# First product of two squared-ReLU MLPs by one level of Strassen's algorithm, their activations through DRAM

## The chip, the core and the metric

The kernel runs on one core of one Trainium2 chip. The metric is the device time of one execution in microseconds (us). Three runs of the kernel before took 2856.18, 2854.34 and 2856.22 us; the median is 2856.18 us.

## What is computed

An encoder trunk of two layers on 1024 tokens with 1024 features, in float32. Each layer is a token mixer and an MLP, both with a pre-RMSNorm and a residual add:

```python
def rmsnorm(x, w):
    y = xf * lax.rsqrt(jnp.mean(xf * xf, axis=-1, keepdims=True) + EPS)
    return y * w
def sq_relu_mlp(h, w1, w2):          # w1: 1024 x 4096, w2: 4096 x 1024
    a = jax.nn.relu(h @ w1)
    return (a * a) @ w2
h = x
h = h + neighbourhood_attention(rmsnorm(h, na_norm), na_w_qkv, na_rpb, na_w_o)
h = h + sq_relu_mlp(rmsnorm(h, mlp_norm[0]), mlp_w1[0], mlp_w2[0])
h = h + gated_deltanet(rmsnorm(h, gdn_norm), gdn_w_in, ..., gdn_w_o)
h = h + sq_relu_mlp(rmsnorm(h, mlp_norm[1]), mlp_w1[1], mlp_w2[1])
return rmsnorm(h, final_norm)
```

## The kernel before, in words

Features lie on the 128 partitions and tokens along the free dimension, so a feature tile is 128 x 1024 and is worked on in two halves of 512 tokens. Every float32 operand is split into two float32r tiles, `hi` (a rounded copy) and `lo` (the rest), and a product of 128 x 128 weights with 128 x 512 tokens is three matmuls: hi hi, hi lo, lo hi (`product`, line 120, its matmul on line 132). ScalarE (ACT) makes `hi`, VectorE (DVE) makes `lo`.

Weights come by `weight` (line 91): per 512 rows x 128 columns one DMA of 256 KB on SyncE's queue (SP) into a `wraw` buffer (three), then `split_w` (line 104): a cast to `whi` on ACT (line 108) and a subtraction to `wlo` on DVE (line 109), with three buffers each. One such split is used by 4 k-tiles x 3 matmuls x 2 halves = 24 matmuls.

The order of the instructions on each engine is not the order of the program text: the framework schedules by the program's order as priority, and an instruction whose inputs and buffers are ready is put ahead of an earlier one that is not. What has a buffer to go to can run ahead.

Around the MLPs the work is staged so. `out_proj` (line 509) makes the mixer's output projection: 8 feature tiles x 2 halves; in layer 0 over 8 k-tiles, in layer 1 over the last 2 heads only (the other six were added to the residual in DRAM during the mixer). The residual tiles `h` (8 tiles of 512 KB) were brought from DRAM by `unspill` (line 527). Each half is added from PSUM to `h` on DVE (line 518), and `norm_tile` (line 142) makes hi (ACT, line 152) and lo (DVE, line 153) of gain * h, the squares (ACT, line 163) and their running sum on GpSimd (POOL, line 164). The factor 1/sqrt(mean) per token, being the same for all features, is only put in after the first product: `norm_end` (line 194) with its sums over partitions (line 178), a power on POOL (line 170) and its spread over the partitions (line 190).

`mlp` (line 198) takes 4 blocks of 1024 hidden features. A block first makes 8 hidden tiles: for each tile and half, 24 matmuls with `w1`, then `max(ps, 0) * rstd` (DVE, line 221), its square as `ahi` (ACT, line 222), the square once more on POOL (line 223) and `alo` (DVE, line 224). The hidden tiles stay in SBUF, in one of two sets of 16 slots called X and A (the other holds the MLP's input). Then the block makes its part of the second product, 8 output tiles x 2 halves x 24 matmuls with `w2`, and adds each to `h` (DVE, line 250; in the last block `after` follows with the next norm, the spill to DRAM or, in layer 1, the final norm and the output).

Either product of one MLP is 32 x 2 x 24 = 1536 matmuls. PSUM has 8 banks: two `mm` banks rotate for the products, two `pa` banks serve the norms.

## Time and profile before

| what | value |
|---|---|
| median of three runs | 2856.18 us |
| span of the profiled execution (no other time of it is given) | 2853.0 us |
| PE busy | 2782.4 us, 14844 matmuls |
| DVE busy | 1377.4 us, 2905 instructions |
| ACT busy | 938.7 us, 2111 instructions |
| POOL busy | 604.7 us, 871 instructions |
| DMA | 177.13 MB, mean 62 GB/s |

PE is TensorE's matmul, PEld its weight load. A row of the windows view gives, for a stretch of the span in us from its start, its length, then the busy time and the instructions of PE, PEld, DVE, ACT and POOL, the granted clock of TensorE, the DMA engines' busy share and the rate. A row of the groups gives line, engine, operation, out<-in, count, then busy us and mean ns of one, then the idle time before them and what ended it. A row of the timeline gives start, duration, engine, line, operation and count. Neighbouring matmuls overlap in the records, so the pace of PE is read from counts in a stretch, not from the duration of one.

MLP 0's `out_proj` runs from about 525 to 605 us, its blocks to about 1335 us; MLP 1's `out_proj` begins at 2076.5 us, its blocks about 2111 us.

### The profile page before, as it was taken

Reading aid. Unit: us, or ns where it says so; the run is one execution under the profiler, and the core shown is the slowest. Engines: PE = TensorE matmul, PEld = TensorE weight load, DVE = VectorE, ACT = ScalarE, POOL = GpSimd, SP = SyncE. Lnnn points to the kernel's source line nnn. Section 1 sums busy time; section 2 is a strip of 40 time slices with the busy share of each in tenths; the row PEclk is TensorE's granted clock in tenths of the full one; section 3 lists DMA queues with packets and bytes.
Section 4 is the critical chain, followed back from the end, with each engine's and each line's share of the span. In section 5 each row is a group of like instructions: output and inputs, shape, how many; then the busy total and the mean of one; then the engine's idle time right before and its main releaser. Section 6 shows DMA issues by size and latency. Waiting matters only on the chain. (4 is left out here: it accounts for less than half of the span.)

```text
span 2853.0 us, 39344 instructions
## 1 busy us (share of the span) xinstructions
PE 2782.4 (98%) x14844; PEld 2198.5 (77%) x14844; DVE 1377.4 (48%) x2905; ACT 938.7 (33%) x2111; POOL 604.7 (21%) x871
## 2 busy tenths in 40 slices
PE   8999999999999999999998999899989999999998
PEld 6766666788888888877777878787868888888887
DVE  5155556433232232334767888887563232232333
ACT  5144444332121121223445555455342121121134
POOL 0101111121010010112155545543142011020111
PEclk9999999999999999999999999999999999999999
DMA  7212212221111111123112222114331111111123
GB/s 194 53 44 58 52 45 51 96 60 49 48 45 51 45 48 49 45 71 91 43 41 51 53 53 50 43 43 117 114 117 50 45 48 49 45 49 48 45 70 115
DMA packets 308588, 177.13 MB, mean 62 GB/s; under 512 B 75054, under 2 KB 286638, under 8 KB 308398
## 3 DMA queue, kind: packets, MB, share of 16 engines
q1 hardware_dynamic: 299982, 166.13, 20.6%
q0 software_dynamic: 3072, 8.39, 1.3%
q8 instruction: 117, 1.92, 0.3%
q10 hardware_dynamic: 5344, 0.09, 0.1%
q14 instruction: 73, 0.60, 0.1%
HBM read 141.62 MB, written 24.55 MB: 58 GB/s over the span
## 5 line engine op out<-in xcount | busy, mean ns | idle before, releaser
L132 PE MATMUL mm<-X,whi 128*128 128x512 f32 x2800 | 902.2, 400 | 0.9 <-ACT X L499 0.7
L132 PE MATMUL mm<-A,whi 128*128 128x512 f32 (+1 forms) x2124 | 669.9, 396 | 3.3 <-ACT whi L108 1.9
L132 PEld LDWEIGHTS mm<-X,whi 128*128 128x128 f32 x2800 | 525.3, 188 | 132.2 <-issue 7.5
L132 PE MATMUL mm<-X,wlo 128*128 128x512 f32 x1400 | 559.7, 400 | 0.0
L132 PEld LDWEIGHTS mm<-A,whi 128*128 128x128 f32 x2124 | 398.9, 189 | 100.0 <-ACT whi L108 2.9
L108 ACT CAST whi<-wraw 128x512 fp32r<-128x512 f32 (+1 forms) x338 | 208.0, 616 | 792.6 <-PE mm L132 760.1
L132 PE MATMUL mm<-A,wlo 128*128 128x512 f32 (+1 forms) x1062 | 419.8, 396 | 2.5 <-DVE wlo L109 2.5
L1189 PE MATMUL mm<-A,whi 128*128 128x512 f32 x1216 | 404.5, 413 | 1.1 <-DVE A L1189 1.1
L223 POOL TENSOR_TENSOR r<-r 128x512 f32<-128x512 f32 x128 | 152.1, 1188 | 1104.6 <-DVE r L221 1098.5
L109 DVE TENSOR_TENSOR wlo<-wraw,whi 128x512 fp32r<-128x512 f32 (+1 forms) x338 | 243.3, 721 | 199.0 <-ACT whi L108 198.6
L132 PEld LDWEIGHTS mm<-X,wlo 128*128 128x128 f32 x1400 | 263.8, 188 | 63.0 <-issue 1.7
L1189 PEld LDWEIGHTS mm<-A,whi 128*128 128x128 f32 x1216 | 214.8, 191 | 41.4 <-DVE A L1189 1.9
L1189 PE MATMUL mm<-A,wlo 128*128 128x512 f32 x608 | 241.6, 397 | 0.0
L132 PEld LDWEIGHTS mm<-A,wlo 128*128 128x128 f32 x1062 | 200.6, 189 | 50.3 <-DVE wlo L109 3.4
L221 DVE SCALAR_TENSOR_TENSOR r<-mm,rs 128x512 f32<-128x512 f32 x128 | 88.5, 691 | 287.7 <-PE mm L132 286.8
L250 DVE TENSOR_TENSOR h<-mm,h 128x512 f32<-128x512 f32 x111 | 76.7, 691 | 300.4 <-PE mm L132 300.4
L1189 POOL TENSOR_TENSOR xt<-lp,xi 128x126 f32<-128x126 f32 (+22 forms) x248 | 110.4, 445 | 174.5 <-DMA lp<-dsc 155.7
L1189 DVE SCALAR_TENSOR_TENSOR X<-xp,cw,X 128x512 f32<-128x512 f32 x192 | 141.9, 780 | 1.7 <-ACT X L1189 1.0
L1189 PEld LDWEIGHTS mm<-A,wlo 128*128 128x128 f32 x608 | 115.3, 190 | 28.0
L164 POOL TENSOR_TENSOR rs<-rs,r 128x512 f32<-128x512 f32 x55 | 75.7, 1381 | 269.0 <-ACT r L163 268.7
L1189 POOL TENSOR_TENSOR xi<-xi,xt 128x126 f32<-128x126 f32 (+22 forms) x248 | 112.6, 454 | 19.4
L222 ACT ACTIVATE X<-r 128x512 fp32r<-128x512 f32 x64 | 40.6, 634 | 170.6 <-DVE r L221 170.6
(264 smaller groups left out, 3148.7 us busy)
## 6 DMA issues: line engine op xcount, KB each, us to landing
wraw<-in_mlp_w_dram SPq DMA_DIRECT2D x276, 256.0 KB
wraw<-in_gdn_w_in_dram SPq DMA_DIRECT2D x64, 256.0 KB
wraw<-in_na_w_qkv_dram SPq DMA_DIRECT2D x32, 256.0 KB
h<-hs SPq DMA_DIRECT2D x16, 512.0 KB
wraw<-in_na_w_o_dram SPq DMA_DIRECT2D x20, 256.0 KB
A<-in_x_dram SPq DMA_DIRECT2D x16, 256.0 KB
wvraw<-in_na_w_qkv_dram SPq DMA_DIRECT2D x8, 512.0 KB
hs<-A SPq DMA_DIRECT2D x16, 256.0 KB
```

Source lines behind the costliest of these rows:

```text
L108: nc.scalar.copy(out=hi[:, :nk], in_=raw[:, :nk])
L109: nc.vector.tensor_tensor(out=lo[:, :nk], in0=raw[:, :nk], in1=hi[:, :nk].bitcast(FP32), op=ALU.subtract)
L132: nc.tensor.matmul(out=ps, lhsT=a, rhs=b, start=n == 0, stop=n == last)
L164: nc.gpsimd.tensor_tensor(out=st["acc", half], in0=st["acc", half], in1=sq, op=ALU.add)
L221: nc.vector.scalar_tensor_tensor(out=r, in0=ps, scalar=0.0, in1=st["rstd", half], op0=ALU.max, op1=ALU.mult)
L222: nc.scalar.activation(out=ahi[:, sl], in_=r, func=AF.Square)
L223: nc.gpsimd.tensor_tensor(out=q, in0=r, in1=r, op=ALU.mult)
L250: nc.vector.tensor_tensor(out=hv, in0=ps, in1=hv, op=ALU.add)
L1189: r = f(*args, **kw)
```

## The change

For two hidden tiles at a time (a quad: 2 output tiles x 2 halves of the tokens, with even and odd k-tiles as the inner halves), the first product is made from 7 block products of 4 k-tiles x 3 matmuls instead of 8. The seven token-side operands per even/odd pair of feature tiles are made once per MLP, in `out_gather` and, for the later pairs, in the first quad; they take all 16 slots of one set, 7 of the other and 5 work tiles. The four weight sums of each quad are made on POOL. The 7 products go through PSUM adds on DVE and two adds on POOL to 4 hidden half tiles, which are multiplied by `rstd`, squared in float32 and stored to a DRAM tile `hidden` (2048 bytes per partition and store). After all 16 quads the second product runs over 4 blocks, whose hidden tiles come back from DRAM (512 KB each) and are split then, for the next block while the present one is multiplied; the first block's eight are loaded in the last quad, as its operands are done with. The residual is no longer kept in SBUF from `out_proj` on: it is read half by half, stored again, and loaded for the second product by `unspill`. Weights of a quad come by two DMAs of 512 KB. The `pa` banks in the first phase are one instead of two.

```diff
+    def block(self, name, group, rest, spare, y, wo, gain, early, order, w1, w2, after, **how):
+        def late(j):
+            for f in {1: (0,), 5: (1, 2), 2: (3,), 6: (4, 5), 3: (6,), 7: (7,)}.get(j, ()):
+                a.append(self.hidden_tile(group, 0, f))
+        with self.phase(name + "a", 1):
+            get = self.operands(group, rest)
+            with self.inner(name + "h"):
+                todo = self.out_gather(y, wo, gain, st, get, spare, early, order)
+            with self.inner(name + "w"):
+                self.mlp_first(st, w1, get, other, todo, late)
+        with self.phase(name + "b"):
+            self.unspill()
+            self.mlp_second(a, (group, other), w2, after, **how)
+    ORDER = (1, 5, 2, 6, 3, 7, 4)
+    def halves(self, t, src, g=None):
+        if g is None:
+            nc.scalar.copy(out=t[:, :HALF], in_=src)
+            nc.vector.tensor_tensor(out=t[:, HALF:], in0=src, in1=t[:, :HALF].bitcast(FP32), op=ALU.subtract)
...
+    def gather(self, d, half, hv, gain, get, raw, late):
+        nc, i, g = self.nc, d // 2, gain[:, d:d + 1]
+        if half == 0:
+            j, r = (2, raw(i, 4)) if d % 2 else (1, raw(i, 7))
+            nc.scalar.activation(out=r, in_=hv, func=AF.Copy, scale=g)
+            self.halves(get(j, i), r)
+        elif d % 2 == 0:
+            nc.vector.scalar_tensor_tensor(out=raw(i, 5), in0=hv, scalar=g, in1=raw(i, 7), op0=ALU.mult, op1=ALU.subtract)
+            late[5].append(lambda: self.halves(get(5, i), raw(i, 5)))
+        else:
+            self.halves(get(3, i), hv, g)
+            nc.vector.scalar_tensor_tensor(out=raw(i, 6), in0=hv, scalar=g, in1=raw(i, 5), op0=ALU.mult, op1=ALU.subtract)
+            late[6].append(lambda: self.halves(get(6, i), raw(i, 6)))
+            def last(j):
+                nc.gpsimd.tensor_tensor(out=raw(i, j), in0=raw(i, j), in1=raw(i, 6), op=ALU.subtract)
+                self.halves(get(j, i), raw(i, j))
+            for j in (7, 4):
+                late[j].append(lambda j=j: last(j))
+    def out_gather(self, y, wo, gain, st, get, spare, early, tail):
...
+            hv = self.wk2.tile([P, HALF], FP32, tag="hr", name=self.uid("hr"), bufs=5)
+            nc.sync.dma_start(out=hv, in_=old[d][:, half * HALF:(half + 1) * HALF])
+            ps = self.product(w[d], y, half)
+            nc.vector.tensor_tensor(out=hv, in0=ps, in1=hv, op=ALU.add)
+            self.sumsq(d, half, hv, st)
+            self.spill(d, hv, half)
+            self.gather(d, half, hv, gain, get, raw, late)
+            if d // 2 < early:
+                for j in (5, 6, 7, 4):
+                    for f in late.pop(j, ()):
+                        f()
...
+            for out, x, y, op in ((s1, a21, a22, ALU.add), (s2, s1, a11, ALU.subtract), (s4, a12, s2, ALU.subtract), (s3, a21, a11, ALU.subtract)):
+                nc.gpsimd.tensor_tensor(out=out, in0=x, in1=y, op=op)
...
+            def finish(t, f, half):
+                nc.vector.scalar_tensor_tensor(out=t, in0=t, scalar=0.0, in1=st["rstd", half], op0=ALU.max, op1=ALU.mult)
+                nc.scalar.activation(out=t, in_=t, func=AF.Square)
+                nc.sync.dma_start(out=self.hidden[2 * n + f][:, half * HALF:(half + 1) * HALF], in_=t)
...
+            for j in self.ORDER:
+                hi, lo = [self.sb.tile([P, 4, P], F32R, tag=tag, name=self.uid(tag), bufs=3) for tag in ("whi", "wlo")]
+                nc.scalar.copy(out=hi, in_=left[j])
+                nc.vector.tensor_tensor(out=lo, in0=left[j], in1=hi.bitcast(FP32), op=ALU.subtract)
+                if n == 0:
+                    for f in todo[j]:
+                        f()
+                pool, tag, bufs = {1: (self.pw, "p1", 1), 5: (self.pw, "p5", 1), 2: (self.ps, "mm", 2), 7: (self.ps, "mm", 2)}.get(j, (self.pw, "pq", 3))
+                ps = pool.tile([P, HALF], FP32, tag=tag, name=self.uid(tag), bufs=bufs)
+                for i in range(4):
+                    x = get(j, i)
+                    for m, (u, v) in enumerate(((hi, 0), (hi, HALF), (lo, 0))):
+                        nc.tensor.matmul(out=ps, lhsT=u[:, i], rhs=x[:, v:v + HALF], start=i == 0 and m == 0, stop=i == 3 and m == 2)
+                if n == 0 and j == 5:
+                    rcol = [self.rstd_cols(st, half) for half in range(2)]
+                if n == 0 and j == 2:
+                    for half in range(2):
+                        self.spread(st, half, rcol[half])
+                if j == 1:
+                    p1 = temp(7)
+                    nc.scalar.copy(out=p1, in_=ps)
+                elif j == 5:
+                    p5 = temp(14)
+                    nc.scalar.copy(out=p5, in_=ps)
+                elif j == 2:
+                    finish(add(self.half("r2"), ps, p1), 0, 0)
+                elif j == 6:
+                    u2 = add(temp(15), ps, p1)
+                elif j == 3:
+                    t = add(self.half("r"), ps, p5)
+                    finish(add(t, t, u2, nc.gpsimd), 0, 1)
+                elif j == 7:
+                    add(p1, ps, u2)
+                    finish(add(self.half("r"), p5, p1, nc.gpsimd), 1, 1)
+                else:
+                    finish(add(self.half("r2"), ps, p1), 1, 0)
+                if n == nq - 1:
+                    late(j)
+    def hidden_tile(self, group, b, f):
+        hi, lo = self.pair(group, f)
+        nc.sync.dma_start(out=lo.bitcast(FP32), in_=self.hidden[b * ND + f])
+        nc.scalar.copy(out=hi, in_=lo.bitcast(FP32))
+        nc.vector.tensor_tensor(out=lo, in0=lo.bitcast(FP32), in1=hi.bitcast(FP32), op=ALU.subtract)
...
+    t.block("mlp0", "A", [f"X{i}" for i in range(7)], None, y, a["na_w_o"][0], g_m0, 3, 2, a["mlp_w1"][0], a["mlp_w2"][0], after, reorder=True)
...
+    t.block("mlp1", "X", [f"A{i}" for i in (0, 1, 2, 3, 4, 5, 8)], [f"A{i}" for i in (9, 10, 11, 12)], y, a["gdn_w_o"][0][SPLIT * P:], g_m1, 1, 3, a["mlp_w1"][1], a["mlp_w2"][1],
+            lambda d, half, hv, part=None: t.final_tile(d, half, hv, g_fin, fin, part), tail=ND, cut=True)
```

More of the change, by code (lines that the diff above doesn't have):

```diff
@@ L195, in norm_end @@
         self.spread(st, half, self.rstd_cols(st, half))
-    def mlp(self, st, w1, w2, after, reorder=False, tail=2, cut=False):
-        nc = self.nc
-        x = [st["x"][d] for d in range(ND)]
-        group = "X" if st["group"] == "A" else "A"
-        nblk = w1.shape[1] // D
-        for b in range(nblk):
-            a = []
-            for f in range(ND):
-                c0 = b * D + f * P
-                w = self.weight(w1[:, c0:c0 + P])
-                ahi, alo = self.pair(group, f)
-                if b == 0 and f == 0:
-                    self.norm_end(st, 0)
-                for half in range(2):
-                    sl = slice(half * HALF, (half + 1) * HALF)
-                    ps = self.product(w, x, half)
-                    if b == 0 and f == 0:
-                        if half == 0:
-                            rcol = self.rstd_cols(st, 1)
-                        else:
-                            self.spread(st, 1, rcol)
-                    r = self.half("r")
-                    q = self.half("r2")
-                    nc.vector.scalar_tensor_tensor(out=r, in0=ps, scalar=0.0, in1=st["rstd", half], op0=ALU.max, op1=ALU.mult)
-                    nc.scalar.activation(out=ahi[:, sl], in_=r, func=AF.Square)
-                    nc.gpsimd.tensor_tensor(out=q, in0=r, in1=r, op=ALU.mult)
-                    nc.vector.tensor_tensor(out=alo[:, sl], in0=q, in1=ahi[:, sl].bitcast(FP32), op=ALU.subtract)
-                a.append((ahi, alo))
@@ new lines, with operands, get @@
+    ORDER = (1, 5, 2, 6, 3, 7, 4)
+    def operands(self, group, rest):
+        own = [(j, i) for j in self.ORDER[:5] for i in range(3)] + [(7, 2)]
+        names = dict(zip(own, [f"{group}{i}" for i in (0, 8, 1, 9, 2, 10, 3, 11, 4, 12, 5, 13, 6, 14, 7, 15)]))
+        names.update({(j, 3): n for j, n in zip(self.ORDER, rest)})
+        tiles = {}
+        def get(j, i):
+            if (j, i) not in tiles:
+                tiles[j, i] = self.slot(names[j, i], F32R) if (j, i) in names else self.work(f"t{j}{i}", dt=F32R)
+            return tiles[j, i]
+        return get
@@ new lines, in out_gather, with raw @@
+    def out_gather(self, y, wo, gain, st, get, spare, early, tail):
+        nc = self.nc
+        old, w, late, tiles = self.hs, {}, defaultdict(list), {}
+        def raw(i, j):
+            if (i, j) not in tiles:
+                if spare and i in (1, 2):
+                    k = "spare", j
+                    if k not in tiles:
+                        tiles[k] = self.slot(spare[(5, 6, 7, 4).index(j)], shape=[P, 2, HALF])
+                    tiles[i, j] = tiles[k][:, i - 1]
+                else:
+                    tiles[i, j] = self.wk2.tile([P, HALF], FP32, tag=f"raw{j}", name=self.uid("raw"), bufs=1)
+            return tiles[i, j]
+        for n, (d, half) in enumerate(self.sequence(tail)):
+            if d not in w:
+                w = w if len(y) < 4 else {}
+                w[d] = self.weight(wo[:, d * P:(d + 1) * P])
+            hv = self.wk2.tile([P, HALF], FP32, tag="hr", name=self.uid("hr"), bufs=5)
[9 more added lines that the diff above has]
+                        f()
+        return late
@@ L230, in mlp @@
             for d, half in self.sequence(tail if last else 0):
+                if not last and half:
+                    nxt.append(self.hidden_tile(groups[(b + 1) % 2], b + 1, d))
                 if w[0] != d:
@@ L1477, in trunk, with after @@
     st, fin = {"x": {}, "group": "A"}, {}
[L1478 to L1488 removed]
+    def after(d, half, hv):
+        t.norm_tile(d, half, hv, g_gdn, st)
+        t.spill(d, hv, half)
+    t.block("mlp0", "A", [f"X{i}" for i in range(7)], None, y, a["na_w_o"][0], g_m0, 3, 2, a["mlp_w1"][0], a["mlp_w2"][0], after, reorder=True)
+    first = t.weight(a["gdn_w_in"][0][:, D:D + P])
     with t.phase("gdn"):
```

56 lines of the change are left out of this document (42 added, 14 removed).

## The prediction

> **What bounds the kernel now.** I read the page first (busy times, chain), then the windows, to find the pace of TensorE inside the MLPs, then the groups, the waits and the timelines around the places that the change touches.
>
> ```profile
> span 2853.0 us, 39344 instructions
> PE 2782.4 (98%) x14844; PEld 2198.5 (77%) x14844; DVE 1377.4 (48%) x2905; ACT 938.7 (33%) x2111; POOL 604.7 (21%) x871
> ...
> PE 34%; POOL 7%; DVE 3%; issue 2%; DMA 2%; ACT 1%; SPq 0%; POOLq 0%; ACTq 0%; DVEq 0%
> PE mm L132 25%; PE mm L1189 4%; POOL xi L1189 3%; POOL xt L1189 3%; PE pa L1189 2%; PE ch L1189 1%; DVE X L1189 1%; DMA lp<-dsc 1%; DMA dsc<-ld 0%; POOL ss L1189 0%; ACT ch L1189 0%; DVE ld L1189 0%; DVE X L153 0%; DVE L L1189 0%; PE po L1189 0%
> ```
>
> TensorE is busy for 98% of the span, and the chain's largest item is the product on line 132. A busy TensorE need not be at its pace, so the windows decide: counts in stretches, some inside an MLP and two at the start of MLP 1 (columns: stretch, length, PE, PEld, DVE, ACT, POOL, clock, DMA share, GB/s).
>
> ```profile
> 606.00:700.00 94.00, 93.52 (x415) 75.65 (x415) 32.97 (x51) 21.88 (x35) 21.14 (x18) 1.00 0.16 46
> 700.00:1000.00 300.00, 300.00 (x1288) 241.70 (x1287) 86.64 (x130) 46.89 (x75) 26.03 (x22) 1.00 0.16 47
> 1000.00:1100.00 100.00, 100.00 (x430) 80.60 (x429) 31.13 (x47) 17.98 (x29) 13.32 (x11) 1.00 0.16 48
> 2060.00:2080.00 20.00, 19.59 (x100) 15.87 (x99) 13.61 (x33) 5.87 (x19) 1.64 (x1) 1.00 0.61 193
> 2076.50:2110.50 34.00, 27.86 (x97) 19.54 (x95) 31.43 (x41) 20.07 (x38) 16.96 (x11) 0.90 0.42 147
> 2110.50:2121.00 10.50, 8.11 (x44) 6.67 (x45) 6.42 (x8) 3.52 (x7) 6.37 (x5) 1.00 0.22 62
> ```
>
> From 700 to 1000 us TensorE never rests: 1288 matmuls in 300 us are 0.2329 us each, and 430 in 100 us are the same. There the number of matmuls is the time. At the start of MLP 1 it is not: 96 matmuls of the output projection would need 96 x 0.2329 = 22.4 us and take 34, while DVE is busy for 31.4 of the 34.
>
> **The change, part by part.**
>
> *Matmuls removed.* A quad (two hidden tiles, both halves) has 8 x 12 = 96 matmuls before and 7 x 12 = 84 after; 16 quads in each of two MLPs save 2 x 16 x 12 = 384. Same shape, same weight load before each: 384 x 0.2329 = 89.4 us less, if TensorE stays as full. A quad then lasts 84 x 0.2329 = 19.56 us, a block product 2.79 us.
>
> *The steady quad.* What the other engines then have to do goes by these groups:
>
> ```profile
> L108 ACT CAST whi<-wraw 128x512 fp32r<-128x512 f32 (+1 forms) x338 | 208.0, 616 | 792.6 <-PE mm L132 760.1
> L109 DVE TENSOR_TENSOR wlo<-wraw,whi 128x512 fp32r<-128x512 f32 (+1 forms) x338 | 243.3, 721 | 199.0 <-ACT whi L108 198.6
> L223 POOL TENSOR_TENSOR r<-r 128x512 f32<-128x512 f32 x128 | 152.1, 1188 | 1104.6 <-DVE r L221 1098.5
> L221 DVE SCALAR_TENSOR_TENSOR r<-mm,rs 128x512 f32<-128x512 f32 x128 | 88.5, 691 | 287.7 <-PE mm L132 286.8
> L164 POOL TENSOR_TENSOR rs<-rs,r 128x512 f32<-128x512 f32 x55 | 75.7, 1381 | 269.0 <-ACT r L163 268.7
> L222 ACT ACTIVATE X<-r 128x512 fp32r<-128x512 f32 x64 | 40.6, 634 | 170.6 <-DVE r L221 170.6
> ```
>
> ACT: 7 casts, 2 copies out of PSUM, 4 squares, 13 x about 0.62 = 8.1 us. DVE: 7 `lo` subtractions, 5 adds out of PSUM, 4 max-and-multiply, 16 x 0.70 = 11.2 us. POOL: 4 weight sums and 2 adds of two different tiles; the nearest row is line 164, 1.38 us, so 8.3 us. All are under 19.56 us. DMA: 1.05 MB of weights in and 1.05 MB of hidden tiles out, 2.1 MB / 19.56 us = 107 GB/s, while 193 GB/s were moved from 2060 to 2080 us. Cost: nothing, as long as the weight split stays ahead. That is the thin place: a split fed 24 matmuls (5.6 us) and now feeds 12 (2.8 us), with the same three buffers. The buffer for product j is free when product j-3 has ended, two products or 5.59 us ahead; cast and subtraction take 0.62 + 0.72 = 1.34 us, which leaves 4.2 us for queueing. That a cast isn't queued behind an epilogue shows here (timeline of ACT, MLP 0):
>
> ```profile
> 640.41 0.62 ACT L108 CAST whi<-wraw 128x512 fp32r<-128x512 f32 x1 [1.25 <-PE mm L132]
> 643.21 0.62 ACT L108 CAST whi<-wraw 128x512 fp32r<-128x512 f32 x1 [2.18 <-PE mm L132]
> 644.12 0.63 ACT L222 ACTIVATE X<-r 128x512 fp32r<-128x512 f32 x1 [0.29 <-DVE r L221]
> 649.72 0.63 ACT L222 ACTIVATE X<-r 128x512 fp32r<-128x512 f32 x1 [4.97 <-DVE r L221]
> ```
>
> The casts of the next tile's weights stand ahead of the squares of the present tile, and wait for TensorE to free a buffer, not for data.
>
> *DVE against POOL.* What could lengthen those 11.2 us shows at the start of MLP 1 (groups of 2076 to 2125 us, then single instructions of DVE and POOL):
>
> ```profile
> L153 DVE SCALAR_TENSOR_TENSOR X<-h,g_m,X 128x512 fp32r<-128x512 f32 x16 | 18.8, 1178 | 0.0
> L518 DVE TENSOR_TENSOR h<-mm,h 128x512 f32<-128x512 f32 x15 | 10.2, 682 | 2.3 <-PE mm L132 2.3
> ```
> ```profile
> 2083.15 0.74 DVE L153 SCALAR_TENSOR_TENSOR X<-h,g_m,X 128x512 fp32r<-128x512 f32 x1
> ...
> 2089.08 1.17 DVE L153 SCALAR_TENSOR_TENSOR X<-h,g_m,X 128x512 fp32r<-128x512 f32 x1
> ...
> 2112.71 1.78 DVE L109 TENSOR_TENSOR wlo<-wraw,whi 128x512 fp32r<-128x512 f32 x1
> ```
> ```profile
> 2084.66 9.82 POOL L164 TENSOR_TENSOR rs<-rs,r 128x512 f32<-128x512 f32 x6 [13.35 <-ACT r L163]
> ...
> 2109.03 6.60 POOL L164 TENSOR_TENSOR rs<-rs,r 128x512 f32<-128x512 f32 x4 [4.21 <-ACT r L163]
> ```
>
> While POOL adds, a DVE instruction that reads two SBUF tiles takes 1.17 to 1.78 us instead of 0.74; one that reads PSUM and one SBUF tile stays at 0.68. In a quad 11 of DVE's 16 are of the first kind. At 1.178 each DVE needs 5 x 0.69 + 11 x 1.178 = 16.4 us: still under 19.56, so I keep this at nothing and put the worst row into a rival. The Trainium skill (SBUF — State Buffer, section Who interferes with whom) gives a rule that speaks against this change, which adds weight sums on POOL: a VectorE instruction with two SBUF inputs and a GpSimd instruction that reads SBUF exclude each other for a whole instruction. The rows agree. By that rule a quad could at worst string both engines together, 5 x 0.69 + 11 x 0.69 + 6 x 1.38 = 19.3 us, and the sum would stay as it is.
>
> *Start of MLP 0.* One output-projection half is 24 matmuls or 5.6 us, with up to 4 DVE instructions each: hidden. Its last pair's operands are made in the first quad, several products ahead of their use. The norm's chain lost under 0.5 us before (606 to 700 us). I take +1 us, bounds 0 (there is not even 0.5 us to win) and +4 (a product waits once for a chain of four such steps).
>
> *Start of MLP 1.* Here DVE is the bound. In the output projection it gets 24 two-tile instructions in place of 16 (one for each of 8 first halves, one for 4 even and two for 4 odd second halves, four more for the first pair's late operands): 8 x 1.178 = +9.4 us. In the first quad 12 late operands and 7 weight splits want 19 x 1.178 = 22.4 us of DVE ahead of the last product, against 19.56 us: +2.8. Given back: product 1 needs first halves only and can run before the output projection ends, -2.8 us, and the norm factors are awaited only behind later products:
>
> ```profile
> PE pa L190 <- POOL rcol L170: 2.3, 1, 2.3
> ```
>
> -2.3 us. Together +7 us; bounds 0 (TensorE's rests there are filled by products 1 and 5) and +14 (nothing given back).
>
> *Handover from first to second product, twice.* New: the first block's 8 hidden tiles, 4.2 MB, come from DRAM while the last quad runs. The first can start when product 1 of that quad has freed its operands, 6 x 2.79 = 16.8 us ahead of the quad's end. At 193 GB/s they take 21.7 us, so the last lands 5.0 us into the second product, is cast (1024 columns, twice 0.62 = 1.2 us), and is wanted after 7 x 3 matmuls, at 4.9 us: 1.3 us late; its `lo`, another 1.4 us behind and wanted one matmul later, adds 1.2. I take +3 us each. Bounds: 0 (the DMA moves faster, its share was only 0.61) and +8 (the residual and `w2` tiles mix with them). The residual tiles are wanted 5.6 us in, and two PSUM banks give as much again.
>
> *Second product.* DVE and ACT get 8 splits of 1024 columns per block instead of the old epilogues, and DMA moves 8.4 MB (hidden tiles and `w2`) in a block of 384 x 0.2329 = 89 us, 94 GB/s. Nothing.
>
> *Sum.* The profiled execution spanned 2853.0 us; -89.4 + 1 + 7 + 6 = -75.4 gives 2777.6. The median of the runs lies 3.2 us above the span, so 2781 us. With all added terms at 0 it is 2767, with all at their upper bounds (4 + 14 + 16) 2801.
>
> **The rivals.**
>
> *1. Transfers bunch at the handover.* If hidden tiles, residual (4.2 MB) and `w2` (0.8 MB) go out together, 9.2 MB at 193 GB/s are 47.6 us from 16.8 us ahead: TensorE waits up to 31 us per MLP instead of 3, +56, 2837 us. For it: one queue issues all of them, and half of a set of slots frees late. Against: residual tiles are wanted one per 11 us, the scheduler puts urgent ones first, and from 2060 to 2080 us 193 GB/s went beside a TensorE busy for 19.59 of 20 us.
>
> *2. DVE queues behind POOL.* For products 3 and 7 DVE's max-and-multiply waits for POOL's add. If each time a weight sum stands ahead of that add, DVE stands for 2 x 1.38 us, twice a quad, and the next weight splits are queued behind it: 16.4 + 5.5 = 21.9 us a quad, 2.3 over, x 32 = 75 us: 2856, no change. If only every second time, half of it: 2818. Against: 4.2 us of lead for each split, and DVE only 11.2 us full when POOL is idle.
>
> *3. DVE becomes the bound (slower).* If every two-tile instruction of the steady quads costs what the worst row shows, 1.78 us, DVE needs 5 x 0.69 + 11 x 1.78 = 23.0 us a quad: (23.0 - 19.56) x 32 = +110 us, 2891. It decides for slower from 19.56 + 75.4 / 32 = 21.9 us a quad, that is 1.68 us per such instruction. Against: POOL works 8.3 us of a quad, so it can't be in the way of all 11.
>
> That the matmuls aren't saved at all can't be: the code fixes 84 per quad.
>
> **How the numbers follow.** Chances: forecast with its bounds (2767 to 2801) 0.63; rival 1, wholly or in part (2801 to 2837), 0.12; rival 2 in part (2801 to 2845) 0.11, in full 0.03; rival 3 0.09; better than all bounds (the rests of MLP 1's start fill altogether) 0.02. About 0.2%, 5.7 us, is what a measurement of this kernel can tell from no change. Faster: 0.63 + 0.12 + 0.11 + 0.02 = 0.88; within 0.2%: 0.03; slower: 0.09. The range is 2766 to 2832: below it 0.02, above it rival 3, rival 2 in full and some 0.06 of the partial cases, together 0.2.
>
> **What would show it.** TensorE has 14844 - 384 = 14460 matmuls. In the middle of a first product a 100 us window still has 429 to 430 matmuls, and 16 quads take 313 us. DVE is 11 to 14 us busy per 19.56 us, two-tile instructions between 0.69 and 1.4 us. At the handover TensorE waits about 3 us for `lo` or DMA, once per MLP; at MLP 1's start DVE is over 90% busy from 2077 to about 2140 us. Wrong: fewer than 425 matmuls per 100 us in the quads (rivals 2 and 3: TensorE waiting for `wlo`), or a rest over 8 us at the handover (rival 1).

## The result, and the profile after

The changed kernel took 2803.45 us (median of 4 runs, 2800.76 to 2806.79), the kernel before 2856.07 us on the same chip (4 runs): ratio 0.9822, 95% interval 0.9809 to 0.9836. It is faster, by 52.6 us where the forecast (2781 against 2856.18) had 75.2. The profiled execution spans 2802.7 us, 50.3 less than that of before.

The page of the changed kernel (header, busy times, the chain by engine):

```profile
span 2802.7 us, 39699 instructions
PE 2704.1 (96%) x14460; PEld 2137.0 (76%) x14460; DVE 1603.9 (57%) x3137; ACT 1101.9 (39%) x2375; POOL 765.1 (27%) x951
...
PE 33%; POOL 7%; DVE 4%; DMA 2%; issue 2%; ACT 1%; SPq 0%; POOLq 0%; DVEq 0%; ACTq 0%
```

The 384 matmuls are gone (14460 are left), but TensorE's share fell from 98% to 96%: it now rests. Where, the windows tell (columns as before: stretch, length, PE, PEld, DVE, ACT, POOL, clock, DMA share, GB/s). First the steady quads of both MLPs:

```profile
640.00:880.00 240.00, 240.00 (x1034) 193.05 (x1033) 139.19 (x197) 92.17 (x160) 109.70 (x75) 1.00 0.37 120
700.00:800.00 100.00, 100.00 (x432) 80.43 (x431) 57.63 (x81) 38.15 (x68) 46.11 (x32) 1.00 0.43 137
2300.00:2319.56 19.56, 19.56 (x85) 15.72 (x84) 11.32 (x16) 7.53 (x14) 8.90 (x6) 1.00 0.33 108
```

Here nothing is lost: 1034 matmuls in 240 us are 0.2321 us each, the clock is 1.00, and TensorE waits for nothing between 640 and 900 us. In one quad DVE is busy for 11.3 us, ACT for 7.5, POOL for 8.9 of 19.56. The groups say the same of the weight splits and sums that the change put there:

```profile
L354 DVE TENSOR_TENSOR wlo<-s,whi 128x512 fp32r<-128x512 f32 x128 | 118.8, 928 | 88.4 <-ACT whi L353 88.3
L338 POOL TENSOR_TENSOR s<-quad,quad 128x512 f32<-128x512 f32 x32 | 53.3, 1664 | 17.5 <-DVE wlo L354 17.5
```

The `wlo` subtraction of a weight sum (`s`) takes 0.93 us beside POOL, that of a quad's own weights 0.69, and both are well covered. Now the four places where the MLPs begin and change over; the same stretches of the kernel before come first for the starts (580 to 640 us, and from the begin of MLP 1's output projection, 2076 us there, 2039.5 us after):

```profile
580.00:640.00 60.00, 59.52 (x273) 48.36 (x272) 23.18 (x36) 19.26 (x31) 15.38 (x13) 1.00 0.22 62
2076.00:2166.00 90.00, 81.47 (x342) 63.20 (x342) 54.69 (x74) 34.59 (x60) 33.29 (x24) 0.96 0.27 88
```
```profile
580.00:640.00 60.00, 56.11 (x241) 45.75 (x240) 38.11 (x48) 25.33 (x44) 32.74 (x22) 0.91 0.38 114
2039.50:2129.50 90.00, 69.13 (x257) 52.02 (x256) 75.77 (x90) 45.22 (x82) 56.03 (x37) 0.83 0.49 154
900.00:980.00 80.00, 74.88 (x312) 59.07 (x311) 47.52 (x57) 31.60 (x44) 7.08 (x5) 0.98 0.52 175
2390.00:2470.00 80.00, 72.81 (x293) 57.28 (x292) 44.83 (x53) 29.92 (x42) 4.91 (x4) 0.94 0.54 179
```

A loss is read from counts. At MLP 0's start 273 - 241 = 32 matmuls fewer than before, x 0.2325 us = 7.4 us; at MLP 1's start 342 - 257 = 85, 19.8 us. At the handovers a full TensorE would do 80 / 0.2320 = 345 matmuls: 33 missing are 7.6 us, 52 missing are 12.0 us. Together 46.8 us, where the forecast had 14. The PE column splits each loss in two. MLP 1's start rests 90 - 69.13 = 20.9 us, 12.4 more than before; the other 7.4 us are time in which TensorE counts as busy and does less, with a clock of 0.83. In the same way MLP 0's start lost 3.4 us by rests and 4.0 by the clock, the handovers 5.1 + 2.5 and 7.2 + 4.8: 28 us of rests, 19 us of low clock behind them.

What TensorE waited for at MLP 1's start (releaser: total us, times, longest), and the clock in two short windows:

```profile
PE mm L157 <- DVE hr L305: 7.0, 5, 2.5
PE pa L203 <- POOL rs L189: 5.4, 1, 5.4
PE mm L157 <- ACT X L250: 3.7, 1, 3.7
PE p L363 <- DVE wlo L354: 1.6, 1, 1.6
```
```profile
610.00:620.00 10.00, 7.85 (x29) 6.63 (x29) 5.61 (x6) 2.86 (x5) 9.92 (x8) 0.53 0.43 129
2080.00:2100.00 20.00, 12.38 (x50) 10.28 (x49) 18.59 (x19) 9.00 (x16) 18.01 (x12) 0.67 0.27 84
```

From 2080 to 2100 us DVE and POOL are both nearly full, and the timelines show them in step (start, duration, DVE first, then POOL):

```profile
2083.27 1.78 DVE L254 SCALAR_TENSOR_TENSOR X<-hr,g_m,X 128x512 fp32r<-128x512 f32 x1
2084.97 1.75 DVE L267 SCALAR_TENSOR_TENSOR raw<-hr,g_m,raw 128x512 f32<-128x512 f32 x1
2086.64 0.68 DVE L305 TENSOR_TENSOR hr<-mm,hr 128x512 f32<-128x512 f32 x1
```
```profile
2082.75 1.75 POOL L276 TENSOR_TENSOR A<-A,A 128x512 f32<-128x512 f32 x1
2084.45 1.71 POOL L189 TENSOR_TENSOR rs<-rs,r 128x512 f32<-128x512 f32 x1
```

Each two-tile instruction ends 0.55 us behind the POOL instruction that began just ahead of it, and the next POOL instruction 1.1 us behind that: they take turns. The one DVE instruction that reads PSUM takes 0.68 us. POOL rests just then, but others of its line that lie wholly within POOL additions (at 2064.89, 2067.25 and 2070.74 us) take 0.68 as well.

At MLP 0's handover TensorE waited so (900 to 985 us), and ScalarE's cast for the later of the two `whi` waits stood waiting for its weights from DRAM, which were requested behind the residual tiles:

```profile
PE mm L157 <- ACT whi L133: 3.9, 2, 2.2
PE mm L363 <- DVE wlo L354: 1.2, 1, 1.2
```
```profile
951.93 0.62 ACT L133 CAST whi<-wraw 128x512 fp32r<-128x512 f32 x1 [12.49 <-DMA wraw<-in_mlp_w_dram]
```

The other `whi` wait, 2.2 us, ended with a cast that stood in ScalarE's queue among 1024-column casts of 1.05 us each; so 1.7 of the 5.1 us are a late transfer and the rest queues on ScalarE and VectorE. At MLP 1's handover the two `whi` waits are 5.0 us, the later one (2.8) again behind a transfer.

### The profile page after: what moved, and what is told of

It is laid out like the page before. It is cut to its first block, busy times and chain, and to the rows that moved or that the text cites. A ratio compares the mean times of both kernels' runs of the same rounds, so it can differ in the third digit from the quotient of the medians.

```text
span 2802.7 us, 39699 instructions
## 1 busy us (share of the span) xinstructions
PE 2704.1 (96%) x14460; PEld 2137.0 (76%) x14460; DVE 1603.9 (57%) x3137; ACT 1101.9 (39%) x2375; POOL 765.1 (27%) x951
## 5 line engine op out<-in xcount | busy, mean ns | idle before, releaser
L157 PE MATMUL mm<-X,whi 128*128 128x512 f32 x1792 | 579.1, 399 | 5.9 <-ACT whi L133 5.0
L157 PEld LDWEIGHTS mm<-X,whi 128*128 128x128 f32 x1792 | 335.3, 188 | 87.6 <-issue 7.5
L157 PE MATMUL mm<-A,whi 128*128 128x512 f32 (+1 forms) x1104 | 350.5, 397 | 15.4 <-DVE hr L305 7.0
L157 PE MATMUL mm<-X,wlo 128*128 128x512 f32 x896 | 356.8, 399 | 0.0
L157 PEld LDWEIGHTS mm<-A,whi 128*128 128x128 f32 x1104 | 207.2, 189 | 68.7 <-DVE hr L305 8.1
L1371 PEld LDWEIGHTS mm<-A,whi 128*128 128x128 f32 x1216 | 215.6, 191 | 41.5 <-DVE A L1371 1.9
L134 DVE TENSOR_TENSOR wlo<-wraw,whi 128x512 fp32r<-128x512 f32 (+1 forms) x210 | 155.1, 741 | 128.5 <-ACT whi L133 128.0
L157 PE MATMUL mm<-A,wlo 128*128 128x512 f32 (+1 forms) x552 | 217.7, 395 | 0.1
L157 PEld LDWEIGHTS mm<-X,wlo 128*128 128x128 f32 x896 | 168.7, 188 | 37.6 <-issue 1.7
L354 DVE TENSOR_TENSOR wlo<-s,whi 128x512 fp32r<-128x512 f32 x128 | 118.8, 928 | 88.4 <-ACT whi L353 88.3
L1371 PEld LDWEIGHTS mm<-A,wlo 128*128 128x128 f32 x608 | 115.5, 190 | 28.0
L157 PEld LDWEIGHTS mm<-A,wlo 128*128 128x128 f32 x552 | 104.7, 190 | 24.4 <-DVE wlo L134 0.5
L353 ACT CAST whi<-s 128x512 fp32r<-128x512 f32 x128 | 78.5, 613 | 76.2 <-PE mm L363 50.3
```

What stands on the lines that cost most here:

```text
L134: nc.vector.tensor_tensor(out=lo[:, :nk], in0=raw[:, :nk], in1=hi[:, :nk].bitcast(FP32), op=ALU.subtract)
L157: nc.tensor.matmul(out=ps, lhsT=a, rhs=b, start=n == 0, stop=n == last)
L353: nc.scalar.copy(out=hi, in_=left[j])
L354: nc.vector.tensor_tensor(out=lo, in0=left[j], in1=hi.bitcast(FP32), op=ALU.subtract)
L1371: r = f(*args, **kw)
```

## The experiments

The theory: GpSimd's additions hold VectorE up at the starts, and TensorE stands behind the norm's chain; at the handovers splits and transfers of the second product crowd the last quad. The rival for each is told with its run. The kernels of e1 to e10 ran once each, on three chips on which the kernel before took 2851.8 to 2858.4 us, so their totals say little and the stages are compared. For every run the stages were timed between the same matmuls, counted from the program's first one (added matmuls allowed for); the table gives the difference from the first profile of the changed kernel, in us.

| run | span | MLP 0 start | MLP 0 handover | 980 to 1300 | mixer | MLP 1 start | MLP 1 handover |
|---|---|---|---|---|---|---|---|
| e1_no_sums | 2791.1 | 0.0 | -0.2 | 0.0 | -5.1 | -8.3 | -1.3 |
| e2_norm_later | 2811.5 | -0.2 | -0.3 | +8.8 | -1.5 | +2.5 | +0.4 |
| e3_tied_loads | 2799.0 | -0.4 | +3.1 | -0.1 | -2.9 | -0.2 | -3.4 |
| e4_late_residual | 2797.0 | -0.3 | 0.0 | -0.1 | -2.4 | +0.9 | -5.7 |
| e5_pool_tie | 2802.6 | -0.7 | +2.4 | -0.1 | +2.4 | +0.5 | -2.6 |
| e6_both_halves | 2797.5 | -2.8 | +1.0 | 0.0 | -0.9 | +0.8 | -3.0 |
| e7_fill | 2821.1 | +2.0 | +0.6 | +8.8 | +0.9 | +4.1 | -0.4 |
| e8_part_sums | 2801.0 | -0.4 | +1.2 | 0.0 | -1.5 | +0.2 | -1.9 |
| e9_norm_tied | 2813.8 | +0.5 | +0.5 | +8.8 | -3.6 | +4.0 | -0.1 |
| e10_late_text | 2800.3 | 0.0 | +2.7 | -0.1 | -3.0 | +0.2 | -1.5 |
| e11_combined | 2801.2 | +6.3 | -0.2 | -0.1 | +4.2 | -7.6 | -6.6 |
| e12_after_again | 2808.3 | -0.7 | +0.9 | +8.8 | -2.3 | +1.0 | -0.5 |

Stages that an edit didn't touch tell the scatter: the time ahead of 580 us (not in the table) moves by -1.9 to +3.0 us, the mixer between the MLPs by 5 us either way, MLP 1's handover lies up to 3.4 us below the first profile, the others stay within about 1 us, and the stretch from 980 to 1300 us shows either 0 or +8.8, of which the last run speaks.

**e1_no_sums**

```diff
-            self.sumsq(d, half, hv, st)
+            self.sumsq(d, half, hv, st, len(y) < 4)      # MLP 1 only
...
-            nc.gpsimd.tensor_tensor(out=st["acc", half], in0=st["acc", half], in1=sq, op=ALU.add)
+            if not skip:
+                nc.gpsimd.tensor_tensor(out=st["acc", half], in0=st["acc", half], in1=sq, op=ALU.add)
```

> From the changed kernel, in MLP 1's output projection the running sum of squares on POOL is left out (only the first square of each half is kept, so the norm factors of that MLP are not the reference's); nothing else changes. Theory 'shared port': at MLP 1's start DVE is full because its instructions with two SBUF inputs wait for POOL's additions. Without contention the 49 such instructions between 2039.5 and 2112 us would need 32 us, they took 54; the sums are 22.1 of POOL's 46 us there, so DVE should need about 10 us less, and the kernel should take about 2794 us, with the mean of the two-tile instructions down from 1.17 to about 0.9 us. Rival 'count': DVE simply has too many instructions there, POOL does not matter: the mean stays at 1.1 to 1.2 us and the time within 2 us of 2803.

It took 2792.88 us (before: 2858.42). Without the running sum MLP 1's start is 8.3 us shorter; the mixer's -5.1 us is scatter. The window of its start (columns as above):

```profile
2039.50:2129.50 90.00, 74.32 (x298) 57.30 (x298) 68.89 (x95) 46.98 (x85) 39.43 (x27) 0.89 0.52 165
```

POOL works 39 us instead of 56, DVE gets 95 instructions done instead of 90 in 7 us less, and TensorE makes 41 matmuls more. The instructions with two SBUF inputs that begin from 2039.5 to 2112 us have a mean of 0.89 us (52 of them), where they had 1.13 (47). That POOL's sums hold up this start is shown; what remains is 19.8 - 8.3 = 11.5 us. Which way they do it, by stretching VectorE's instructions or by coming late themselves (the norm waited 5.4 us for the last of them), this run does not separate.

**e2_norm_later**

```diff
-                if n == 0 and j == 5:
+                if n == 0 and j == 6:
                     rcol = [self.rstd_cols(st, half) for half in range(2)]
-                if n == 0 and j == 2:
+                if n == 0 and j == 7:      # spread; what needs the factors is held back until then
...
```

> From the changed kernel, in the first quad of each MLP the sums of the norm come after product 6 instead of 5, their spread after product 7 instead of 2, and the quad's max-and-multiply steps are emitted after that. Theory 'norm chain': with one pa bank, its four steps stand on TensorE and ACT ahead of the products and the weight casts, so that both wait; that is most of the 7.4 us that MLP 0's start lost and some 3 us of MLP 1's. Then MLP 0's start loses 3 us or less, and the kernel takes about 2796 us. Rival 'late operands': the products' operands and weight sums come that late anyway; the stage and the time stay within 2 us.

It took 2813.2 us. Nothing moved at MLP 0's start: the scheduler put the norm's matmuls back to the same place, being ready there. The run tells nothing of the chain; e9 repeats it with a dependence that can't be scheduled away.

**e3_tied_loads**

```diff
-nxt.append(self.hidden_tile(groups[(b + 1) % 2], b + 1, d))
+nxt.append(self.hidden_tile(groups[(b + 1) % 2], b + 1, d, self.h[d]))
...
+        nc.vector.tensor_copy(out=lo[:, 0:1], in_=behind[:, 0:1])      # ahead of the load
```

> From the changed kernel, each hidden tile of the next block is loaded only after the same-numbered output tile of the present block has its first half (a one-column copy on DVE into the tile ties the load to it). Theory 'early splits': at the handover DVE and ACT are full with splits of the second block's tiles, which were put ahead of the last products' weight splits and of the first block's; without them the two handovers lose some 10 us together instead of 19.6, and the kernel takes about 2794 us. Rival 'transfers': w2 and the first block's tiles are late on the DMA queues behind the residual; ACT and DVE have less to do, but the waits stay, and so does the time, within 3 us of 2803.

It took 2800.73 us, and MLP 0's handover was 3.1 us longer, not shorter. The copy stands in DVE's own queue, so a second reason was open; e5 puts it on POOL.

**e4_late_residual**

```diff
+                    if b == 0:      # in mlp_second, behind the w2 weights of tile d, in place of unspill
+                        self.h.append(self.work(f"h{d}"))
+                        nc.sync.dma_start(out=self.h[d], in_=self.hs[d])
```

> From the changed kernel, the residual tile of each output tile is loaded after that tile's w2 weights have been issued, not all eight ahead of the second product. Theory 'transfers': the waits for w2 casts of 1.7 and 2.8 us, 30 us after the handover began, go, with the slow clock behind them: about 5 to 6 us, 2798 us. Theory 'early splits': those waits are small beside the in-order waits on ACT and DVE, the time stays within 2 us of 2803.

It took 2798.75 us: MLP 0's handover unchanged, MLP 1's 5.7 us shorter:

```profile
2390.00:2470.00 80.00, 76.54 (x316) 60.38 (x315) 46.22 (x55) 30.66 (x42) 4.83 (x4) 0.96 0.54 184
```

With the residual loaded one tile at a time, 316 matmuls fit where 293 did, and TensorE waits 2.2 us for `whi` instead of 5.0. The ten runs with the old order show +0.4 to -3.4 us there, -1.4 in the mean, the two with the new one -5.7 and -6.6 (e11). Some 4 to 5 us belong to the edit, with a scatter of about 2.

**e5_pool_tie**

```diff
-            nc.vector.tensor_copy(out=lo[:, 0:1], in_=behind[:, 0:1])      # as in e3
+            nc.gpsimd.tensor_copy(out=lo[:, 0:1], in_=behind[:, 0:1])
```

> In the second product, the load of a hidden tile of the next block is made to wait for a one-column copy on GpSimd that reads the present block's output tile, so that it can't be brought and split during the last quad. (With the copy on VectorE, as in the run before, VectorE itself stood behind these copies.) Theory (splits made too early crowd VectorE and ScalarE at the handover): the 900 to 980 us stretch of MLP 0 gets 3 to 5 us shorter and the waits for whi and wlo at 926 to 930 us vanish. Rival (the late residual and weight transfers are the cost): no change at MLP 0's handover within 1 us. Everything else stays.

It took 2804.32 us (before on that chip: 2851.84), MLP 0's handover 2.4 us longer again. What TensorE waits for from 900 to 985 us:

```profile
PE mm L363 <- DVE wlo L354: 5.3, 1, 5.3
PE mm L157 <- ACT whi L133: 1.2, 1, 1.2
```

The next block's tiles no longer come early, and yet `wlo` of the last quad is late: in this run's timeline DVE reaches it at 927.88 us, behind seven 1.2 us splits of the first block's own tiles. Early tiles of the next block are not the cause. DVE is busy for 38.67 us from 900 to 980 us, where it was 47.52, so the amount of its work is not what counts here; why the order came out worse stays open.

**e6_both_halves**

```diff
-                    rcol = [self.rstd_cols(st, half) for half in range(2)]
+                    bank = lambda: self.pw.tile([P, HALF], FP32, tag="pq", name=self.uid("pq"), bufs=3)
+                    rcol = [self.rstd_cols(st, half, bank() if half else None) for half in range(2)]
...
-                        self.spread(st, half, rcol[half])
+                        self.spread(st, half, rcol[half], bank())
```

> The norm's sums of the second half, and the spreads of both halves, get PSUM banks of their own (of the three pq banks, idle at that time), so that the two halves' chains no longer wait for one pa bank. Theory (the single pa bank strings the chains and TensorE stands behind them): the start of MLP 0 gets 2 to 4 us shorter, 1.7 to 2.5 of it rest and as much again by the clock that falls after the rest; at the start of MLP 1 -1 us, since there the chain waits for GpSimd's running sum. Rival (the late operands of the first quad are what TensorE would wait for anyway): 0, the rest only appears as a wait for products 5 or 2.

It took 2799.19 us. MLP 0's start is 2.8 us shorter, MLP 1's is not:

```profile
610.00:620.00 10.00, 8.50 (x37) 7.54 (x38) 6.18 (x6) 4.55 (x8) 9.91 (x8) 0.72 0.42 122
```

In this window TensorE's rest shrank by only 0.65 us, but it made 37 matmuls instead of 29: one rest of 3.2 us in place of three that add up to 3.9, and a clock of 0.72 instead of 0.53.

**e7_fill**

```diff
+                        for q in range(7):      # behind the sums of each half; idle is a pq bank
+                            nc.tensor.matmul(out=idle, lhsT=hi[:, 0], rhs=get(1, 0)[:, :HALF], start=True, stop=True)
```

> Seven matmuls whose output nobody reads are put behind the norm's sums of each half in the first quad of each MLP, 1.6 us at full pace in a rest of 1.7 and 1.4 us. Theory (half of what the start of MLP 0 lost is the clock that falls after these rests): granted clock from 610 to 620 us rises from 0.53 to over 0.9, and the start of MLP 0 takes 2 to 4 us less although 14 matmuls more are run. Rival (the rest alone costs): no gain, or up to 1.5 us more.

It took 2822.77 us, 2.0 us more at MLP 0's start, 4.1 at MLP 1's, for 14 x 0.2325 = 3.3 us of matmuls each. The rests it was to fill are all still there:

```profile
PE pa L203 <- DVE rcol L194: 1.7, 1, 1.7
PE pa L215 <- POOL rcol L195: 1.4, 1, 1.4
PE pa L215 <- ACT rs L217: 0.8, 1, 0.8
```

The scheduler had put the added matmuls ahead of the sums, so the clock was not tried by this run.

**e8_part_sums**

```diff
+            if len(y) < 4 and d >= 5:
+                nc.scalar.activation(out=st["sq", d][:, half * HALF:(half + 1) * HALF], in_=hv, func=AF.Square)
+            else:
                 self.sumsq(d, half, hv, st)
...
+            for i, t in enumerate([acc] + [the squares of tiles 5 to 7]):
+                nc.tensor.matmul(out=ps[:, j:j + 1], lhsT=t[:, j * P:(j + 1) * P], rhs=self.ones[:, 0:1], start=i == 0, stop=i == 3)
```

> At the start of MLP 1 GpSimd adds the squares of the first five feature tiles only (8 adds for 14); those of the last three stay apart and are summed over the partitions by TensorE together with the running sum (24 single-column matmuls more). Theory (GpSimd's adds stretch VectorE's instructions, and the norm's sums wait 5.4 us for the last of them): the start of MLP 1 gets 4 to 7 us shorter, somewhat less than without any adds (8.3). Rival (leaving the adds out helped only because the norm's chain did not wait any more): 2 us shorter or less once the 24 matmuls are paid.

It took 2802.98 us; MLP 1's start +0.2 us. The wait for the running sum fell from 5.4 to 2.4 us and that for `hr` from 7.0 to 3.2:

```profile
PE mm L157 <- DVE hr L307: 3.2, 2, 2.8
PE pa L205 <- POOL rs L189: 2.4, 1, 2.4
```

But the 24 single-column matmuls are 48 records on TensorE, at the place where its clock is 0.63: the norm's 64 records there take 10.4 us, the 16 of the changed kernel 2.9. The relief came, and was spent at once. The time is the rival's; its reason, that only the norm's wait counts, is not shown by it.

**e9_norm_tied**

```diff
+                        one = self.wk2.tile([P, 1], FP32, tag="one", name=self.uid("one"), bufs=1)
+                        nc.scalar.activation(out=one, in_=p5[:, 0:1], func=AF.Copy, scale=0.0, bias=1.0)
+                        rcol = [self.rstd_cols(st, half, one=one) for half in range(2)]      # sums with this column
...
```

> The column of ones with which the norm's sums over the partitions are made is produced from product 5's evacuated tile (times 0 plus 1), so that these sums can't be put ahead of products 5 and 2; the spread goes behind product 6, and what needs the factors waits for it. TensorE's order is then product 1, product 5, half of product 2, sums, rest of product 2, product 6, spread woven into product 3. Theory (TensorE stands behind the norm's chain because the chain was put ahead of products that had their operands, and then pays again by the lower clock): the start of MLP 0 gets 4 to 7 us shorter, that of MLP 1 6 to 10 us. Rival (VectorE's late operands set the pace there, and TensorE would wait for them instead): 0 to 2 us at either start, the waits for rs, rcol and pa replaced by waits for wlo or the operands.

It took 2815.55 us (before: 2851.83), 8.8 of it from 980 to 1300 us. This time the order on TensorE was the one meant, no wait for `rs`, `rcol` or `pa` is left, and nothing is gained: +0.5 and +4.0 us. The waits at MLP 0's start, then at MLP 1's:

```profile
PE p L367 <- ACT whi L357: 5.8, 1, 5.8
```
```profile
PE p L367 <- ACT whi L357: 11.1, 1, 11.1
PE p L367 <- DVE wlo L358: 6.3, 2, 5.0
```
```profile
2080.00:2100.00 20.00, 9.82 (x34) 6.76 (x33) 20.00 (x19) 11.94 (x22) 14.02 (x10) 0.84 0.36 118
```

DVE is busy for 20.00 of 20 us. My theory of the chain falls: without the norm in its way TensorE waits as long for product 5, so the rival holds, though not quite as it was put. Both waits for `whi` end with ScalarE's cast of a weight sum, which GpSimd made only after its last running sum and operand subtractions (until 611.5 us at MLP 0's start, 2100.1 at MLP 1's). At MLP 1's start, GpSimd and then ScalarE:

```profile
2100.09 1.71 POOL L338 TENSOR_TENSOR s<-quad,quad 128x512 f32<-128x512 f32 x1
```
```profile
2101.83 0.62 ACT L357 CAST whi<-s 128x512 fp32r<-128x512 f32 x1 [1.05 <-POOL s L338]
```

TensorE goes on at 2102.50 us, and the next 5.0 us are for the `wlo` of the same sum, queued on VectorE behind late operands. So the pace of the starts is set by GpSimd and VectorE together: the first quad's weight sums, on GpSimd, come as late as the operands. Why GpSimd did not make this sum in its idle 2.0 us before 2095.26 is not shown.

**e10_late_text**

```diff
-            for f in {1: (0,), 5: (1, 2), 2: (3,), 6: (4, 5), 3: (6,), 7: (7,)}.get(j, ()):
+            for f in range(ND) if j == 4 else ():
```

> The loads and splits of the first block's hidden tiles stand behind the last product of the last quad in the program's order, so that this quad's weight splits go ahead of them; TensorE's order no longer has the second product's first matmuls between products 7 and 4. Theory (an order that mixes the two products makes TensorE wait for splits queued behind 1024-column splits on VectorE): the handover of MLP 0 gets 3 to 5 us shorter and the wait for wlo in the last quad vanishes. Rival (the transfers and the splits of eight tiles are late in any order): within 2 us of the changed kernel's, with a wait for A or DMA at the first matmuls of the second product in place of the wait for wlo. Between kernels whose edit does not touch it MLP 1's handover moved by 1 to 3 us, so MLP 0's is read.

It took 2801.97 us; MLP 0's handover +2.7 us. The last quad runs through now, and one wait stands in place of three:

```profile
PE mm L157 <- DVE wlo L134: 7.5, 1, 7.5
```

At MLP 1's handover the same 7.5 us show. Theory and rival both miss here: the waits in the last quad are gone, but nothing is gained. In either order, the first block's eight tiles want eight `lo` subtractions of 1.22 us on VectorE beside the last quad's epilogues, and TensorE waits for the end of that queue.

**e11_combined**

```diff
-            self.sumsq(d, half, hv, st)
+            nc.scalar.activation(out=sq, in_=hv, func=AF.Square)      # sq is float32r
+            nc.tensor.matmul(out=st["sum", half], lhsT=self.one.broadcast_to([P, P]), rhs=sq, start=d == 0, stop=d == ND - 1)
...
+ the edits of e4_late_residual and e6_both_halves
```

> Three edits together. The running sum of squares leaves GpSimd in both MLPs: ScalarE's square goes as float32r through one matmul with ones per half tile (16 per MLP, 16 x 0.2325 = 3.7 us of TensorE), accumulated in a PSUM bank that is idle then, and copied once to SBUF for the norm's sums; the norm's chains have banks of their own as in the run on that; the residual is loaded tile by tile behind the second product's weights as in the run on that. Theory (GpSimd's adds string VectorE's two-tile instructions, and that sets the pace at both starts): MLP 1's start 6 to 10 us shorter, MLP 0's 3 to 6, MLP 1's handover about 3; 2786 to 2794 us, 0.3 to 0.6% below the changed kernel. Rival (VectorE's and TensorE's own work set the pace, what the adds give back is eaten by the 16 matmuls): MLP 1's start 0 to 3 us shorter, the whole within 6 us of the changed kernel.

It took 2797.27 us (median of 5, 2788.21 to 2803.20), the kernel before 2853.17 on the same chip: ratio 0.9793, 0.9777 to 0.9809. That is above the 2786 to 2794 us expected, yet 16.6 us below the changed kernel on that chip (e12, 0.9857). Between the two profiles 8.9 us of the difference lie in the stretch from 980 to 1300 us, which these edits do not touch (-0.1 here, +8.8 in e12), so what they are worth as a whole is not shown; the stages are read. MLP 1's start is 7.6 us shorter, as expected, its handover 6.6. MLP 0's start is 6.3 us longer, where 3 to 6 less were expected. In its output projection TensorE had no rest to give (columns of the group: count, busy us, mean ns, idle ahead):

```profile
L312 PE MATMUL pq<-r,one 128*128 128x512 f32 x16 | 7.6, 478 | 3.2 <-ACT r L309 3.2
```

The 16 matmuls cost 16 x 0.2325 = 3.7 us there, and 3.2 us of waiting for the squares besides. At MLP 1's start the same 16 fall into rests, and VectorE's instructions are shorter: the group `X<-A,X` of line 251 has a mean of 0.79 us instead of 1.18:

```profile
L253 DVE TENSOR_TENSOR X<-A,X 128x512 fp32r<-128x512 f32 x9 | 7.1, 794 | 0.3 <-ACT X L252 0.3
```
```profile
L251 DVE TENSOR_TENSOR X<-A,X 128x512 fp32r<-128x512 f32 x9 | 10.4, 1177 | 0.0
```

By these stages the sums on TensorE in MLP 1 alone should be the better version; it was not run.

**e12_after_again** (no edit)

> The changed kernel once more, unaltered, beside the run before on the same chip. It tells how far a stage moves by itself from run to run: theory (the last block of MLP 0's second product, whose operand is read with a stride, falls into one of two paces by chance): its matmuls come either every 0.227 us as in the first profile or every 0.249 us as in two of the experiments and in the kernel before, 8 us apart, and the times of single runs scatter accordingly. Rival (the pace belongs to the kernel): 0.227 us again and a scatter of no more than 3 us; the mixers' stage between the MLPs may move by up to 5 us in either case.

The unaltered kernel took 2813.87 us (median of 4, 2809.98 to 2815.03), ratio 0.9857, 0.9844 to 0.9871, against 0.9822 in the first set. The two profiles differ by much more than the scatter in one place, the last block of MLP 0's second product, whose operand is read in runs of 8 elements. One window of it in the first profile, in the second, and in the kernel before:

```profile
1225.00:1265.00 40.00, 40.00 (x178) 33.02 (x177) 15.24 (x22) 13.09 (x21) 9.30 (x7) 1.00 0.32 99
```
```profile
1225.00:1265.00 40.00, 40.00 (x162) 30.23 (x161) 14.42 (x22) 12.72 (x21) 7.95 (x6) 1.00 0.27 86
```
```profile
1265.00:1305.00 40.00, 40.00 (x161) 30.22 (x161) 13.69 (x20) 12.43 (x20) 7.96 (x6) 1.00 0.26 83
```

TensorE is busy all through, the clock is 1.00, and it makes 178 matmuls or 161. One kernel has shown both paces, so the kernel alone does not fix it. The +8.8 us of e2, e7 and e9 in that stretch are the same thing and not their edits, so of the first profile's 50.3 us some 9 were this pace. Nine of the thirteen profiles of the changed kernel and its variants have the fast pace. The one profile of the kernel before has the slow one, and no run of that kernel is below 2851.66 us, so nothing shows it at the fast pace; whether the change makes the fast one likelier is not known. What chooses it stays open: on one chip e1 had the one and e2 the other, while either set of the changed kernel lies within about 6 us and the two medians are 10 us apart. That a set keeps one pace throughout is likely from this, not shown: only one execution of each was profiled.

## Why the prediction was right in sign and too large

**As a whole.** 2803.45 us lie in the range of 2766 to 2832, but 2.5 us outside the forecast's own bounds (2767 to 2801). All four added terms came out larger than forecast, and three of them above their upper bounds. The range held because the rivals had widened it, though rivals 2 and 3 did not happen and rival 1 only in a small part; and 8.8 us of the gain are the pace of the strided block, which no term of the forecast had: for the prediction that was luck. Without it the time would have been about 2812 us.

**Matmuls removed, steady quad, second product: right.** 384 x 0.2329 us were saved, the quads run at 0.2321 us a matmul and the second product at 0.2331 (944 in 220 us from 2470 us on), and rivals 2 and 3 are out: TensorE has no wait between 640 and 900 us, and the dearest two-tile instruction takes 0.93 us where rival 3 needed 1.68.

**Start of MLP 1, +7 forecast, +19.8 measured: the step that failed most.** That GpSimd's additions lengthen this start is shown by e1, and VectorE is full there (e9: 20.00 of 20 us); the price of 1.178 us for such an instruction came out as forecast (1.177 in the group above). Four things were wrong with the sum. The "-2.8" and "-2.3" given back did not come: product 1 begins only behind the last matmul of the output projection (2080.99 us), the norm waited 5.4 us for the running sum, and e9 shows that nothing is gained by moving it. The "+2.8" set the late operands against the end of the first quad, while products 5 and 2 want them near its begin. The weight sums on GpSimd were put at nothing, which holds in the steady quad; in the first quad they come behind GpSimd's other work, and with the chain out of the way TensorE waited 11.1 us for the first of them (e9). And the sum counted rests only, though the clock of 0.90 stood in a row that the prediction quotes: another 7.4 us. The Trainium skill's rule (SBUF — State Buffer, section Who interferes with whom) was weighed in the steady quad alone. At MLP 1's start the trace agrees with it: both engines alternate, at 1.71 to 1.78 us an instruction.

**Start of MLP 0, +1 forecast with a bound of +4, +7.4 measured.** "Hidden" was taken from a kernel in which VectorE was 23 us busy in that stretch of 60 us; after, it is 38, and POOL goes from 15 to 33 us. Rests 3.4 us, low clock 4.0. e6 wins 2.8 of it by other banks; e9 puts a wait for product 5's weight sum in the place of the rest.

**Handover, +3 each forecast, +7.6 and +12.0 measured.** The transfers were priced at 193 GB/s and are not the main thing: the DMA moved up to 377 GB/s in ten microseconds. What was missing are the queues of ScalarE and VectorE, where 8 casts of 1.05 us and 8 splits of 1.22 us come at once among the last quad's own (e5, e10): 3.4 of the 5.1 us of rests at MLP 0, 7.5 us of wait in the order of e10. At MLP 1 the residual's transfers add 4 to 5 us (e4), which is rival 1 in a small part. No run takes the splits themselves away, so their share is read from the waits. The slow matmuls behind the rests, 2.5 and 4.8 us, were not in the sum either.

**The ledger.** -89.4 + 7.4 + 19.8 + 7.6 + 12.0 = -42.6; the strided block's pace gives -8.8, together -51.4 against -50.3 in the profile. The rest is within the scatter of the mixer's stage. With the slow pace on both sides the change is worth about 40 us; the second set has 39.3 (2853.17 - 2813.87), where the pace of the kernel before is not known.

## What to carry to other kernels

A change that takes work from the bound engine is paid back at its edges, where the operands of the first and last round are made: price those, weights as well as inputs, by the engine that makes them, against the first product that wants them. Price a rest of TensorE with the slow matmuls behind it; here 28 us of rests went with a loss of 47. And before an edit gets the credit for a few microseconds, time the stages that it doesn't touch in several profiles: one of them had two paces 8.8 us apart.

## What the runs showed of the hardware

- In two executions of one kernel (the changed one, first profile and e12) the same matmuls (clock 1.00, no wait) with an operand read in runs of 8 elements came every 0.227 us, all alike, or every 0.249 us, varying from 0.228 to 0.270. Contiguous operands gave 0.231 and 0.236 in the kernel before, 0.233 and 0.234 in the changed one. So a strided read was, in the good case, faster than a contiguous one.
- GpSimd's power over 128 x 4 elements did not hold VectorE up as its additions of 128 x 512 did (timeline of the changed kernel, POOL, then DVE beside it: 0.69 us against 1.75 above):

```profile
2087.46 1.51 POOL L195 TENSOR_TENSOR rcol<-rcol,mhalf 128x4 f32<-128x4 f32 x1 [1.30 <-DVE rcol L194]
```
```profile
2088.01 0.69 DVE L251 TENSOR_TENSOR A<-raw,A 128x512 fp32r<-128x512 f32 x1
```

- The clock fell to 0.53 at MLP 0's start though no rest there was longer than 1.74 us (the changed kernel's timeline of TensorE, the norm's matmuls):

```profile
606.78 0.95 PE L203 MATMUL pa<-ones,rs 128*128 128x1 f32 x8
609.47 1.02 PE L203 MATMUL pa<-ones,rs 128*128 128x1 f32 x8 [1.74 <-DVE rcol L194]
611.87 2.08 PE L215 MATMUL pa<-ident,rcol 128*128 128x128 f32 x8 [1.39 <-POOL rcol L195]
614.72 1.62 PE L215 MATMUL pa<-ident,rcol 128*128 128x128 f32 x6 [0.77 <-ACT rs L217]
```

  The Trainium skill (TensorE: Matmul & The Clock Gate, section HAM oscillation — how this bites in real kernels) warns of idle gaps above about 3.4 us; the trace shows that shorter ones, with only small matmuls between them, do it as well.
- The DMA moved 377 GB/s at MLP 1's handover, with TensorE's clock at 1.00 (window of the changed kernel):

```profile
2430.00:2440.00 10.00, 7.70 (x33) 5.86 (x32) 0.74 (x2) 1.12 (x2) 0.00 (x0) 1.00 1.05 377
```
